# A decoder layer on one core: the value projection made wide, turned tiles sent through DRAM, weights loaded from GpSimd's queue, and another order of the value products

## The chip, the cores and the metric

The kernel runs on one core of a Trainium2 chip. The metric is the device time of one execution in microseconds, lower is better. The engines are named as the profile names them: PE is TensorE (PEld its weight loads), DVE is VectorE, ACT is ScalarE, POOL is GpSimd, and SP is SyncE, which here only issues DMAs.

## The reference, cut to what matters

The reference is one decoder layer over 2048 tokens of width 1024, in float32. The input is normalised and multiplied by one large matrix, whose columns give the inputs of two groups of heads. The first group has four HGRN2 heads: a recurrence whose state is a 128 x 128 matrix for each head. The second has eight attention heads of width 64 over two key and value heads, with a window of 128 tokens and a learned sink in the softmax. Both outputs are normalised or weighted, joined, multiplied by an output matrix and added to the input. Then follow a gated MLP with a causal convolution of three taps, a residual sum and a last normalisation.

```python
u = rmsnorm(h, norm_mix_w)
proj = u @ w_in                      # hq, hf, hi, hg and the attention's q, k, v
# an HGRN2 head, token by token, with k_t = 1 - f_t and v_t from hi:
#   S_t = diag(f_t) S_(t-1) + k_t v_t^T,   o_t = S_t^T q_t
# an attention head:
p = jnp.exp(scores - m)
denom = jnp.sum(p, axis=-1, keepdims=True) + jnp.exp(sink - m)
out = jnp.einsum('bnhgqk,bnkhd->bnqhgd', p / denom, vb)
```

The change concerns `hi`, the values of the HGRN2 heads (512 of the columns of `w_in`), and the way in which some tiles are turned from tokens on partitions to features on partitions or back.

## The kernel before, in words

The 2048 tokens are worked in two halves of 1024. In each half the mixing stage comes first (projections, HGRN2 heads, attention), then the output projection, the gate and up projections, and the down projection.

The normalised input lies in SBUF with the 1024 features on partitions, eight tiles of 128 x 1024 tokens. Each tile is kept as two parts, XH (rounded to the format of fast float32 products) and XL (what the rounding left). A weight is split in the same way: `prep` (L192) loads 128 x 1024 floats (512 KB) into `raw`, a ring of three buffers, by a DMA of SP (L198); ACT casts it to the high part (L199, whi), DVE subtracts (L200, wlo). The two parts have rings of two buffers each. A projection of 128 columns is a `unit` (L203): 48 products of 128 x 512 (L218), that is eight feature tiles, three combinations of high and low parts, and two blocks of 512 tokens, into two PSUM banks. The ring `mm` of PSUM banks has four.

The HGRN2 values are not a `unit`. `project_v` (L670) works on two heads at once: for each of eight tiles of 128 tokens it makes 24 products of 128 x 256 (L681 to L683), with the tokens' tile as the stationary operand and the weight as the moving one, so that the result `pvv` has tokens on partitions. ACT copies it out in 16 activations that scale each token by its `rs` (L685). There are 192 such products in a call, 768 in the program.

The order of the mixing stage is a list, `ORDER` (L40). Its entries are f, q, l, s, p for an HGRN2 head (forget gate, query, seven levels, state, product), qa, sc, pv, pw for a pair of attention heads (query projection, scores and softmax, value products of the first and of the second block of 512 tokens), v for a value projection, g for a gate and m for a split. The list is the order in which the code is written; a scheduler then settles the order on each engine, so that neighbouring stages mix. Within one engine, and on SP's and POOL's queues, the settled order is kept: an instruction that waits holds up those behind it.

A level of an HGRN2 head multiplies the tiles Q and K by gates on DVE (L564, L565), makes small products on PE (plev, L558 and L572), and copies part of them under a mask into ST (L584). ST is cleared first by a memset of POOL (L507). The levels' small products are float32 and stand between the wide products of whichever projection runs at the time.

The attention's softmax tile `sc` has queries on partitions; its value products need keys there. For pairs 0 to 2 `turned` (L335) turns it: DVE transposes blocks of 32 x 32 (L338), and SP issues 16 DMAs of 32 KB from SBUF to SBUF (L341) that put the blocks in their places in `pt`. Then DVE picks out the part of `pt` that belongs to a block's own tokens (po, L453), and PE makes the value products (poT, L471) from `pt` and `po`. The outputs of heads 0 to 2 (`on`) are turned by the same function into `hg`. Pair 3 and head 3 are turned by PE instead. So there are 12 tiles `pt` and 6 tiles `hg` in the program.

Of the kernel before, what the change touches and what calls it, by code (L numbers as in the profile page):

```python
# [17 lines left out]
P = 128  # L18
# [20 lines left out]
UP_AFTER = 'T2'  # L39
ORDER = ("f0 q0 l0 qa0 v0 sc0 s0 p0 f1 q1 pv0 pw0 l1 qa1 sc1 f2 s1 p1 q2 pv1 pw1 l2 qa2 v1 sc2 f3 s2 p2 q3 pv2 "  # L40
         "pw2 l3 qa3 sc3 s3 p3 pv3 pw3 g0 g1 m4 m5 m6 g2 m0 m1 g3 m7 m2 m3").split()
LEVELS = [1, 2, 4, 8, 16, 32, 64]
# [4 lines left out]
TURNED_PAIRS = 3  # L47
TURNED_HEADS = 3


@with_exitstack
def hymba_layer(ctx: ExitStack, tc: tile.TileContext, a: dict, out: bass.AP, rows_out: bass.AP):
# [139 lines left out]
    def prep(src, slots=False, parts=(slice(0, D),)):  # L192

        raw = raw4(None)
        hi, lo = [hp.tile([P, D], F32R, tag="m", name=f"w{t}", bufs=KT) if slots else
                  wp.tile([P, D], F32R, tag=t, name=f"w{t}", bufs=2) for t in ("hi", "lo")]
        for c in parts:
            nc.sync.dma_start(raw[:, c], src[:, c])  # L198
            nc.scalar.copy(hi[:, c], raw[:, c])  # L199
            nc.vector.tensor_tensor(lo[:, c], raw[:, c], hi[:, c].bitcast(F32), op=ALU.subtract)  # L200
        return hi, lo
# [132 lines left out]

    def turned(p, tag, bufs, src, dst):  # L335

        t = p.tile([P, 4, 8, 32], F32, tag=tag, name="turn", bufs=bufs)
        nc.vector.transpose(t, src.rearrange("p n (c j) -> p c n j", j=32))  # L338
        for a in range(4):
            for c in range(4):  # L340
                nc.sync.dma_start(dst[32 * c:32 * c + 32, a], t[32 * a:32 * a + 32, c])  # L341

    def rows(kv):
        return slice(kv * HD, (kv + 1) * HD)
# [38 lines left out]
    def attend(hf, j, X, invb, KS, V, VD, mix, p):  # L383
# [9 lines left out]
        for g in range(NB):  # L393
# [48 lines left out]
            if j < TURNED_PAIRS:  # L442
                pt = p.tile([P, 4, 8, 32], F32, tag="sc", name="pt", bufs=2)
                turned(p, "pp", 3, sc.rearrange("p a b c -> p (a b) c"), pt)
                sc = pt
# [39 lines left out]
    def hgrn(hf, h, X, invb, vs, WG, gates, mix, p, fu=None):  # L485
# [114 lines left out]
        kept = TT if hf + 1 < NH else TT - 1  # L600
        Kn = p.tile([P, TT, P], F32, tag="t4", name="Kn", bufs=2)
        for b in range(NB):
            pk = ps("hg", "pkn")
            n = min(4, kept - 4 * b)
            for i in range(n):
                c = slice((b * 4 + i) * P, (b * 4 + i + 1) * P)
                nc.tensor.transpose(pk[:, i * P:(i + 1) * P], K[:, c], ident)
            nc.scalar.copy(Kn[:, 4 * b:4 * b + n].rearrange("p a b -> p (a b)"), pk[:, 0:n * P])
        SS = p.tile([P, TT, P], F32, tag="SS", name="SS", bufs=1)
        for b in range(NB):  # L610
            pu = ps("hg", "pu")
            for c in range(4 * b, min(4 * b + 4, kept)):
                i = c % 4
                marks["pu"] = nc.tensor.matmul(pu[:, i * P:(i + 1) * P], Kn[:, c], v[:, c], start=True, stop=True)
            for c in range(4 * b, min(4 * b + 4, kept)):
# [13 lines left out]
        for b in range(NB):  # L629
            at = [po[b][:, i * P:(i + 1) * P] for i in range(4)]  # L630
            empty = hf == 0 and b == 0
            for i in range(4):
                for k in range(2):
                    marks["po"] = nc.tensor.matmul(at[i][rows(k)], ST[:, k, 4 * b + i], v[:, 4 * b + i],
                                                   start=i == 0, stop=empty and i == 0, skip_group_check=True)
# [15 lines left out]
        if h < TURNED_HEADS:  # L651
            turned(p, "t4", 2, on, q.rearrange("p (a c q) -> p a c q", a=4, c=TT))
        for b, bs in halves() if h >= TURNED_HEADS else ():
# [15 lines left out]

    def project_v(hf, pr, X, rs, p):  # L670

        v = [p.tile([P, TT, P], F32, tag="v", name="v", bufs=VB) for _ in range(2)]
        parts = [prep(a["w_v"][pr, s]) for s in range(2)]
        for tt in range(TT):
            o = ps("mm", "pvv")
            t = slice(tt * P, (tt + 1) * P)
            for kt in range(KT):
                hi, lo = parts[kt // 4]
                xh, xl = X[kt]
                c = slice((kt % 4) * 256, (kt % 4 + 1) * 256)  # L680
                nc.tensor.matmul(o[:, 0:256], xh[:, t], hi[:, c], start=kt == 0, stop=False)  # L681
                nc.tensor.matmul(o[:, 0:256], xl[:, t], hi[:, c], start=False, stop=False)  # L682
                nc.tensor.matmul(o[:, 0:256], xh[:, t], lo[:, c], start=False, stop=kt == KT - 1)  # L683
            for i in range(2):
                nc.scalar.activation(v[i][:, tt], o[:, i * P:(i + 1) * P], AF.Identity, scale=rs[:, tt:tt + 1])  # L685
        return v
# [467 lines left out]
    for hf in range(NH):  # L1154
        X, kv, invb, rs, f0 = nxt
        with ExitStack() as st:
# [7 lines left out]
            for name in ORDER:  # L1164
# [9 lines left out]
                elif stage == "v":  # L1174
                    vs += project_v(hf, n, X, rs, p)
                else:
# [10 lines left out]
def _layout(i):  # L1187
# [3 lines left out]
    def cols(w, idx):  # L1191
# [12 lines left out]
    w_out = i["w_out"][0][np.concatenate(rows)]  # L1204
    w_v = np.stack([cols(w_in, 1024 + pr * 256 + ar(256)).reshape(P, 2, D).transpose(1, 0, 2) for pr in range(2)])
    conv = np.concatenate([i["conv_w"][0], i["conv_b"]], 0)
# [5 lines left out]
        "w_f": np.stack([cols(w_in, 512 + h * P + ar(P)) for h in range(4)]),  # L1212
        "w_v": w_v,
        "w_g": np.stack([cols(w_in, 1536 + h * P + ar(P)) for h in range(4)]),
# [39 lines left out]
```

## Time and profile before

| | |
|---|---|
| time, median of 3 runs | 2129.19 us (2128.93 to 2129.2) |
| time of the profiled execution | 2129.44 us |
| span of its trace | 2127.7 us |
| TensorE clock granted in the profiled execution | 0.999 of full speed |
| TensorE busy | 99% of the span |
| VectorE, ScalarE, GpSimd busy | 77%, 49%, 1% |

The span runs from the first instruction of the trace to the last, 1.7 us less than the execution's own time. In a row of the timeline the first number is the start in us from the span's start, the second how long the row lasts, then engine, line, operation, the tiles written and read, the shape, and after x the number of instructions that the row joins; brackets hold the idle time of the engine just before it and what ended that. Durations of products on TensorE overlap: the next starts before the last has drained. SPq is SP's queue, where a row lasts as long as the issue takes; the DMA itself lands later, and the list of DMA issues gives the count, the KB of each and the median us from issue to landing.

### The profile page before, as it was taken

What the parts mean: (1) busy time and instruction counts of PE and PEld (TensorE: products, weight loads), DVE (VectorE), ACT (ScalarE), POOL (GpSimd) and SP (SyncE); (2) the same over time, 40 slices, a digit from 0 to 9 for tenths busy, and PEclk for the clock granted to TensorE, in tenths of its full rate; (3) what the DMA queues carried; (4) which work ended last, traced back from release to release, by engine and by line L of the source; (5) the groups of instructions that cost most, each with busy time, mean ns of one, the idle gap of its engine ahead of it and who ended that gap; (6) DMA issues with size and microseconds to landing.
All of it is one profiled execution on the core that took longest, in us unless ns stands there. A gap on an engine that the chain in (4) does not pass through costs nothing.

```text
span 2127.7 us, 30275 instructions
## 1 busy us (share of the span) xinstructions
PE 2113.7 (99%) x11575; PEld 1763.0 (83%) x11575; DVE 1632.4 (77%) x2427; ACT 1050.0 (49%) x1855; POOL 16.9 (1%) x43
## 2 busy tenths in 40 slices
PE   8999999999999999999999999999999999999998
PEld 6988888888888888888889898888888888888887
DVE  6587786798887878785865776867988788887765
ACT  5455645564444445335635456555544444453353
POOL 2000000000000000000000000000000000000000
PEclk9999999999999999999999999999999999999999
DMA  4121213413232335964641212242223323259644
GB/s 162 42 59 45 68 52 102 136 59 121 91 124 92 98 116 168 379 235 150 216 143 40 61 38 64 60 146 97 80 99 103 110 90 124 94 194 403 228 149 134
DMA packets 105810, 264.34 MB, mean 124 GB/s; under 512 B 15808, under 2 KB 28608, under 8 KB 105664
## 3 DMA queue, kind: packets, MB, share of 16 engines
q1 hardware_dynamic: 105232, 262.14, 36.6%
q8 instruction: 91, 1.49, 0.3%
q14 instruction: 55, 0.45, 0.1%
q10 hardware_dynamic: 432, 0.27, 0.0%
HBM read 195.56 MB, written 57.34 MB: 119 GB/s over the span
## 4 chain that ended last, share of the span: by engine, by line
PE 97%; DVE 2%; DMA 1%; ACT 0%; issue 0%; SPq 0%; ACTq 0%; DVEq 0%
PE X L818 7%; PE X L816 7%; PE X L817 7%; PE pop L218 7%; PE hq L218 4%; PE q L218 4%; PE g L218 4%; PE f L218 4%; PE Y L817 4%; PE Y L818 4%; PE Y L816 4%; PE pdx L1004 3%; PE pdx L1003 3%; PE pdx L1005 3%; PE pdy L1004 3%; PE pdy L1003 3%
## 5 line engine op out<-in xcount | busy, mean ns | idle before, releaser
L689 ACT CAST whi<-raw 128x1024 fp32r<-128x1024 f32 x88 | 92.7, 1053 | 115.1 <-PE X L817 73.1
L816 PE MATMUL X<-T,whi 128*128 128x512 f32 x352 | 136.9, 389 | 0.0
L817 PE MATMUL X<-T,whi 128*128 128x512 f32 x352 | 136.9, 389 | 0.0
L818 PE MATMUL X<-T,wlo 128*128 128x512 f32 x352 | 136.9, 389 | 0.0
L887 DVE SCALAR_TENSOR_TENSOR y<-ga,cw,y 128x1024 f32<-128x1024 f32 x88 | 112.5, 1279 | 25.9 <-ACT y L885 25.9
L822 ACT COPY u<-X 128x512 f32<-128x512 f32 x88 | 51.5, 585 | 122.8 <-PE X L818 122.6
L690 DVE TENSOR_TENSOR wlo<-raw,whi 128x1024 fp32r<-128x1024 f32 x88 | 107.2, 1218 | 4.4 <-ACT whi L689 4.4
L199 ACT CAST whi<-raw 128x1024 fp32r<-128x1024 f32 x58 | 60.6, 1050 | 89.9 <-PE pop L218 36.7
L690 DVE TENSOR_TENSOR xld<-raw,xhd 128x1024 fp32r<-128x1024 f32 x72 | 80.9, 1131 | 18.3 <-ACT xhd L689 18.2
L689 ACT CAST xhd<-raw 128x1024 fp32r<-128x1024 f32 x72 | 70.0, 978 | 37.6 <-DMA raw<-act0T 12.0
L218 PE MATMUL pop<-XL,whi 128*128 128x512 f32 x256 | 82.8, 390 | 0.0
L218 PE MATMUL pop<-XH,wlo 128*128 128x512 f32 x256 | 82.6, 390 | 0.0
L218 PE MATMUL pop<-XH,whi 128*128 128x512 f32 x256 | 82.5, 391 | 0.0
L200 DVE TENSOR_TENSOR wlo<-raw,whi 128x1024 fp32r<-128x1024 f32 x58 | 70.5, 1217 | 10.4 <-ACT whi L199 10.1
L818 PEld LDWEIGHTS X<-T,wlo 128*128 128x128 f32 x352 | 66.1, 188 | 13.8
L817 PEld LDWEIGHTS X<-T,whi 128*128 128x128 f32 x352 | 66.1, 188 | 13.7
L816 PEld LDWEIGHTS X<-T,whi 128*128 128x128 f32 x352 | 66.0, 188 | 13.7
L682 PE MATMUL pvv<-whi,XL 128*128 128x256 f32 x256 | 72.7, 285 | 0.0
L681 PE MATMUL pvv<-whi,XH 128*128 128x256 f32 x256 | 72.6, 285 | 0.0
L683 PE MATMUL pvv<-wlo,XH 128*128 128x256 f32 x256 | 72.4, 287 | 0.0
L818 PE MATMUL X<-B,wlo 128*128 128x512 f32 x176 | 68.7, 390 | 0.8 <-DVE wlo L690 0.8
L817 PE MATMUL X<-T,Sh 128*128 128x512 f32 x176 | 68.6, 390 | 0.5 <-DVE T L690 0.5
(388 smaller groups left out, 6287.9 us busy)
## 6 DMA issues: line engine op xcount, KB each, us to landing
wr<-in_w_down SPq DMA_DIRECT2D x90, 512.0 KB, 5.6
raw<-in_w_gate SPq DMA_DIRECT2D x44, 512.0 KB, 3.6
raw<-in_w_up SPq DMA_DIRECT2D x44, 512.0 KB, 3.6
raw<-act0T SPq DMA_DIRECT2D x20, 512.0 KB, 5.6
raw<-act1T SPq DMA_DIRECT2D x20, 512.0 KB, 5.9
act0B<-y SPq DMA_DIRECT2D x33, 256.0 KB, 2.4
act1B<-y SPq DMA_DIRECT2D x33, 256.0 KB, 2.4
raw<-in_w_out SPq DMA_DIRECT2D x16, 512.0 KB, 3.7
```

The lines of the kernel that those rows point to most:

```text
L218: nc.tensor.matmul(o[b], w, x[:, bs], start=f, stop=l)
L681: nc.tensor.matmul(o[:, 0:256], xh[:, t], hi[:, c], start=kt == 0, stop=False)
L682: nc.tensor.matmul(o[:, 0:256], xl[:, t], hi[:, c], start=False, stop=False)
L683: nc.tensor.matmul(o[:, 0:256], xh[:, t], lo[:, c], start=False, stop=kt == KT - 1)
L689: nc.scalar.copy(h, src)
L690: return (eng or nc.vector).tensor_tensor(l, src, h.bitcast(F32), op=ALU.subtract)
L816: nc.tensor.matmul(o, wh[:, ws], xh, start=i == 0 and not more, stop=False, skip_group_check=more)
L817: nc.tensor.matmul(o, wh[:, ws], xl, start=False, stop=False, skip_group_check=more)
L818: nc.tensor.matmul(o, wl[:, ws], xh, start=False, stop=i == 3, skip_group_check=more)
L887: nc.vector.scalar_tensor_tensor(y, g[:, w:w + HALF], C.cw[:, ft, w:w + 1], y, op0=ALU.mult, op1=ALU.add)
L1003: nc.tensor.matmul(o, wh[:, i, c], ah[:, i, cols], start=f, stop=False, skip_group_check=more)
L1004: nc.tensor.matmul(o, wh[:, i, c], al[:, i, cols], start=False, stop=False, skip_group_check=more)
```

## The change

The value projection is now a `unit` for one head: 48 products of 128 x 512 with the weight as the stationary operand, 384 in the program. Its result `vT` has the head's 128 features on partitions and lies in two PSUM banks. DVE transposes both banks in blocks of 32 x 32, the tile goes through `turned` into `v`, and eight activations of ACT scale it in place. `v` is laid out as 4 groups of 32 features with the token tiles between them, and the products that read it (pu and po of the HGRN2 heads) take it in four pieces of 32 elements.

`turned` makes one DMA of 512 KB from SBUF into a DRAM tile (`turned`, four buffers) and four DMAs of 128 KB back, each for 32 partitions. It serves 26 tiles: the 12 `pt`, the 6 `hg` and 8 `v`. SP's 288 transfers of turned tiles become 130: 26 writes, 48 reads of `pt`, 24 of `hg`, 32 of `v`.

`prep` issues its DMA from POOL's queue where it was SP's. That concerns 58 loads; the weights of gate, up and down are loaded elsewhere and stay with SP.

`ORDER` has four v entries where it had two, in other places, and for pairs 0 to 2 the value products stand behind the levels of the next head; for pairs 0 and 1 they stand behind the next pair's query projection too. A branch for turned keys is added and is not taken (`TURNED_KEYS` is 0). In the changed kernel the lines behind `turned` are numbered some ten higher (L453 is L463, L471 is L481, L584 is L594), those of `prep` one higher.

```diff
-ORDER = ("f0 q0 l0 qa0 v0 sc0 s0 p0 f1 q1 pv0 pw0 l1 qa1 sc1 f2 s1 p1 q2 pv1 pw1 l2 qa2 v1 sc2 f3 s2 p2 q3 pv2 "
-         "pw2 l3 qa3 sc3 s3 p3 pv3 pw3 g0 g1 m4 m5 m6 g2 m0 m1 g3 m7 m2 m3").split()
+ORDER = ("f0 q0 l0 qa0 v0 v1 sc0 s0 p0 f1 q1 l1 qa1 pv0 pw0 sc1 f2 s1 p1 q2 l2 qa2 v2 pv1 pw1 v3 sc2 f3 s2 p2 q3 l3 pv2 pw2 qa3 sc3 s3 p3 pv3 pw3 g0 g1 m4 m5 m6 g2 m0 m1 g3 m7 m2 m3").split()
...
+DB = 4
...
-            nc.sync.dma_start(raw[:, c], src[:, c])
+            nc.gpsimd.dma_start(raw[:, c], src[:, c])
...
-    def turned(p, tag, bufs, src, dst):
+    def turned(p, tag, bufs, src, dst, strided=False):
 
         t = p.tile([P, 4, 8, 32], F32, tag=tag, name="turn", bufs=bufs)
-        nc.vector.transpose(t, src.rearrange("p n (c j) -> p c n j", j=32))
-        for a in range(4):
-            for c in range(4):
-                nc.sync.dma_start(dst[32 * c:32 * c + 32, a], t[32 * a:32 * a + 32, c])
+        tv = t.rearrange("p c n i -> p c (n i)").rearrange("p c (i n) -> p c n i", n=8) if strided else t
+        for i, s in enumerate(src):
+            n = 8 // len(src)
+            nc.vector.transpose(tv[:, :, i * n:(i + 1) * n], s.rearrange("p (n c j) -> p c n j", n=n, j=32))
+        d = dp.tile([P, 4, 256], F32, tag="turned", name="turned", bufs=DB)
+        nc.sync.dma_start(d.rearrange("p c x -> p (c x)"), flat(t))
+        for c in range(4):
+            nc.sync.dma_start(dst[32 * c:32 * c + 32].rearrange("p a b c -> p a (b c)"),
+                              d[:, c].rearrange("(a j) x -> j a x", a=4))
...
-                marks["pu"] = nc.tensor.matmul(pu[:, i * P:(i + 1) * P], Kn[:, c], v[:, c], start=True, stop=True)
+                marks["pu"] = nc.tensor.matmul(pu[:, i * P:(i + 1) * P], Kn[:, c], v[:, :, c], start=True, stop=True)
...
-    def project_v(hf, pr, X, rs, p):
-
-        v = [p.tile([P, TT, P], F32, tag="v", name="v", bufs=VB) for _ in range(2)]
-        parts = [prep(a["w_v"][pr, s]) for s in range(2)]
-        for tt in range(TT):
-            o = ps("mm", "pvv")
-            t = slice(tt * P, (tt + 1) * P)
-            for kt in range(KT):
-                hi, lo = parts[kt // 4]
-                xh, xl = X[kt]
-                c = slice((kt % 4) * 256, (kt % 4 + 1) * 256)
-                nc.tensor.matmul(o[:, 0:256], xh[:, t], hi[:, c], start=kt == 0, stop=False)
-                nc.tensor.matmul(o[:, 0:256], xl[:, t], hi[:, c], start=False, stop=False)
-                nc.tensor.matmul(o[:, 0:256], xh[:, t], lo[:, c], start=False, stop=kt == KT - 1)
-            for i in range(2):
-                nc.scalar.activation(v[i][:, tt], o[:, i * P:(i + 1) * P], AF.Identity, scale=rs[:, tt:tt + 1])
+    def project_v(h, X, rs, p):
+
+        o = unit(a["w_v"][h], X, "vT")
+        v = p.tile([P, 4, TT, 32], F32, tag="v", name="v", bufs=VB)
+        turned(p, "pp", 3, o, v)
+        for c in range(TT):
+            nc.scalar.activation(v[:, :, c], v[:, :, c], AF.Identity, scale=rs[:, c:c + 1])
         return v
```

The scheduler's order moves in the whole mixing stage. Three places show what the prediction speaks of.

The first is VectorE in the first half, from the softmax of pair 0's second block on. Before, the names are: `sc` the softmax tile, `turn` its blocks transposed, `po` the first and then the second block's own part, K, Q, ST and F the levels of the next head.

```order
L441 TENSOR_TENSOR sc<-sc,den 128x1024
L338 STREAM_TRANSPOSE turn<-sc 128x1024
L453 TENSOR_TENSOR po<-pt,ownT 128x1024
L565 TENSOR_TENSOR Q<-Q,F_1455 128x2x64x4
L584 COPY_PREDICATED ST<-lmask_297,plev 64x2x32x4 x2
L564 TENSOR_TENSOR K<-K,F_1489 128x2x16x16
L490 TENSOR_TENSOR f<-f_1771,invb 128x512
L490 TENSOR_TENSOR f<-f_1772,invb 128x512
L200 TENSOR_TENSOR wlo<-raw,whi 128x1024
L419 MEMSET sc 128x128 x2
L565 TENSOR_TENSOR Q<-Q,F_1472 128x2x32x8
L584 COPY_PREDICATED ST<-lmask_303,plev 64x2x16x8 x2
```

The po of the second block stands four rows behind the last of these, after three small products of F. In the changed kernel, from the same multiplication on:

```order
L451 TENSOR_TENSOR sc<-sc,den 128x1024
L575 TENSOR_TENSOR Q<-Q,F_1305 128x2x64x4
L594 COPY_PREDICATED ST<-lmask_297,plev 64x2x32x4 x2
L346 STREAM_TRANSPOSE turn<-sc 128x1024
L463 TENSOR_TENSOR po<-pt,ownT 128x1024
L574 TENSOR_TENSOR K<-K,F_1339 128x2x16x16
L575 TENSOR_TENSOR Q<-Q,F_1322 128x2x32x8
L594 COPY_PREDICATED ST<-lmask_303,plev 64x2x16x8 x2
L429 MEMSET sc 128x128 x2
L463 TENSOR_TENSOR po<-pt,ownT 128x1024
L500 TENSOR_TENSOR f<-f_1639,invb 128x512
L500 TENSOR_TENSOR f<-f_1640,invb 128x512
```

The transpose now has the level's Q and masked copies ahead of it instead of behind it, and the second block's po (the second L463) stands five rows behind the first where it stood thirteen behind.

The second is TensorE at the same pair: `poT` are the value products, hq and f are projections of the next heads, plev a level's small products. Before, at the start of the second block:

```order
L218 MATMUL hq_1938<-XL,whi 128x512
L218 MATMUL hq_1937<-XH,wlo 128x512
L558 MATMUL plev<-Q,G 64x2x32 x8
L218 MATMUL hq_1938<-XH,wlo 128x512
L471 MATMUL poT<-pt,V 64x128 x2
L218 MATMUL hq_1937<-XH,whi 128x512
L218 MATMUL hq_1938<-XH,whi 128x512
L414 MATMUL psc<-KS,qx 128x128
L218 MATMUL hq_1937<-XL,whi 128x512
L471 MATMUL poT<-po,VD 64x128 x2
L471 MATMUL poT<-pt,V 64x128 x2
```

In the changed kernel, from the end of the first block's products on:

```order
L219 MATMUL f_1639<-XL,whi 128x512
L219 MATMUL f_1640<-XL,whi 128x512
L219 MATMUL f_1639<-XH,wlo 128x512
L219 MATMUL f_1640<-XH,wlo 128x512
L219 MATMUL hq_1795<-XH,whi 128x512
L568 MATMUL plev<-Q,G 64x2x32 x8
L219 MATMUL hq_1796<-XH,whi 128x512
L219 MATMUL hq_1795<-XL,whi 128x512
L219 MATMUL hq_1796<-XL,whi 128x512
L481 MATMUL poT<-pt,V 64x128 x2
L219 MATMUL hq_1795<-XH,wlo 128x512
L219 MATMUL hq_1796<-XH,wlo 128x512
```

The second block begins (poT<-pt) after nine rows of other work behind the first block, where it stood 25 rows behind before; the wide products around it are the same kind.

The third is SP's queue in the first half, where weights, turned tiles of pairs 0 and 1 (`pt`) and of head 0 (`hg`) follow each other. Before:

```order
L373 DMA kcarry<-KS 256x1x128
L374 DMA vcarry<-V 128x128
L198 DMA raw<-in_w_q 128x1024
L198 DMA raw<-in_w_att 128x1024
L198 DMA raw<-in_w_f 128x1024
L198 DMA raw<-in_w_q 128x1024
L198 DMA raw<-in_w_att 128x1024
L341 DMA pt<-turn 32x256 x16
L341 DMA hg_537<-turn 32x256 x16
L198 DMA raw<-in_w_v 128x1024 x2
L341 DMA pt<-turn 32x256 x16
L198 DMA raw<-in_w_f 128x1024
```

In the changed kernel, from the same two rows on:

```order
L383 DMA kcarry<-KS 256x1x128
L384 DMA vcarry<-V 128x128
L348 DMA turned<-turn 128x1024
L350 DMA v<-turned 32x4x256 x4
L348 DMA turned<-turn 128x1024
L350 DMA v<-turned 32x4x256 x4
L348 DMA turned<-turn 128x1024
L350 DMA pt<-turned 32x4x256 x4
L348 DMA turned<-turn 128x1024 x2
L350 DMA pt<-turned 32x4x256 x4
L350 DMA hg_537<-turned 32x4x256 x4
```

The weights are gone from SP, the tiles `v` are new, and a write of one tile can stand ahead of the reads of another. The weights' loads are now on POOL, here from its masks (`lmask`) at the start of the program on:

```order
L117 AFFINE_SELECT lmask_297<-lmask_297 128x64 x2
L117 AFFINE_SELECT lmask_303<-lmask_303 128x64 x2
L199 DMA raw<-in_w_f 128x1024
L117 AFFINE_SELECT lmask_309<-lmask_309 128x64 x2
L119 AFFINE_SELECT lmask_285<-lmask_285 128x64 x2
L119 AFFINE_SELECT lmask_291<-lmask_291 128x64 x2
L119 AFFINE_SELECT lmask_297<-lmask_297 128x64 x2
L119 AFFINE_SELECT lmask_303<-lmask_303 128x64 x2
L119 AFFINE_SELECT lmask_309<-lmask_309 128x64 x2
L199 DMA raw<-in_w_q 128x1024
L199 DMA raw<-in_w_att 128x1024
L199 DMA raw<-in_w_v 128x1024 x2
```

Before, POOL had no load; here the first f weight stands between the selects, the others behind them, and the memset of the first ST behind the second f weight.

More of the change, by code (lines that the diff above doesn't have):

```diff
@@ L48 @@
 TURNED_HEADS = 3
+TURNED_KEYS = 0
+DB = 4
 @with_exitstack
@@ L333, in across, with flat @@
         return bass.AP(v.tensor, v.offset + base, [list(v.ap[0])] + dims)
-    def turned(p, tag, bufs, src, dst):
+    def flat(t):
+        return t.rearrange("p a b c -> p (a b c)")
+    def turned(p, tag, bufs, src, dst, strided=False):
         t = p.tile([P, 4, 8, 32], F32, tag=tag, name="turn", bufs=bufs)
-        nc.vector.transpose(t, src.rearrange("p n (c j) -> p c n j", j=32))
-        for a in range(4):
-            for c in range(4):
-                nc.sync.dma_start(dst[32 * c:32 * c + 32, a], t[32 * a:32 * a + 32, c])
+        tv = t.rearrange("p c n i -> p c (n i)").rearrange("p c (i n) -> p c n i", n=8) if strided else t
[7 more added lines that the diff above has]
+                              d[:, c].rearrange("(a j) x -> j a x", a=4))
     def rows(kv):
@@ L443, in attend @@
                 pt = p.tile([P, 4, 8, 32], F32, tag="sc", name="pt", bufs=2)
-                turned(p, "pp", 3, sc.rearrange("p a b c -> p (a b) c"), pt)
+                turned(p, "pp", 3, [sc.rearrange("p a b c -> p (a b c)")], pt)
                 sc = pt
@@ L600, in hgrn @@
         kept = TT if hf + 1 < NH else TT - 1
-        Kn = p.tile([P, TT, P], F32, tag="t4", name="Kn", bufs=2)
-        for b in range(NB):
+        if h < TURNED_KEYS:
+            Kt = p.tile([P, 4, 32, TT], F32, tag="t4", name="Kt", bufs=2)
+            turned(p, "t4", 2, [K], Kt, True)
+            Kn = Kt.rearrange("p a i n -> p n (a i)")
+        else:
+            Kn = p.tile([P, TT, P], F32, tag="t4", name="Kn", bufs=2)
+        for b in range(NB) if h >= TURNED_KEYS else ():
             pk = ps("hg", "pkn")
@@ L633, in hgrn @@
                 for k in range(2):
-                    marks["po"] = nc.tensor.matmul(at[i][rows(k)], ST[:, k, 4 * b + i], v[:, 4 * b + i],
+                    marks["po"] = nc.tensor.matmul(at[i][rows(k)], ST[:, k, 4 * b + i], v[:, :, 4 * b + i],
                                                    start=i == 0, stop=empty and i == 0, skip_group_check=True)
@@ L651, in hgrn @@
         if h < TURNED_HEADS:
-            turned(p, "t4", 2, on, q.rearrange("p (a c q) -> p a c q", a=4, c=TT))
+            turned(p, "t4", 2, [on.rearrange("p c t -> p (c t)")], q.rearrange("p (a c q) -> p a c q", a=4, c=TT))
         for b, bs in halves() if h >= TURNED_HEADS else ():
@@ L1174, in hymba_layer @@
                 elif stage == "v":
-                    vs += project_v(hf, n, X, rs, p)
+                    vs.append(project_v(n, X, rs, p))
                 else:
@@ L1204, in _layout @@
     w_out = i["w_out"][0][np.concatenate(rows)]
-    w_v = np.stack([cols(w_in, 1024 + pr * 256 + ar(256)).reshape(P, 2, D).transpose(1, 0, 2) for pr in range(2)])
     conv = np.concatenate([i["conv_w"][0], i["conv_b"]], 0)
@@ L1212, in _layout @@
         "w_f": np.stack([cols(w_in, 512 + h * P + ar(P)) for h in range(4)]),
-        "w_v": w_v,
+        "w_v": np.stack([cols(w_in, 1024 + h * P + ar(P)) for h in range(4)]),
         "w_g": np.stack([cols(w_in, 1536 + h * P + ar(P)) for h in range(4)]),
```

## The prediction

> **What bounds the kernel now.** I read the page's engine line first, then its chain of waits, then the waits of TensorE, then the timeline at the places that the change touches.
>
> ```profile
> PE 2113.7 (99%) x11575; PEld 1763.0 (83%) x11575; DVE 1632.4 (77%) x2427; ACT 1050.0 (49%) x1855; POOL 16.9 (1%) x43
> PE 97%; DVE 2%; DMA 1%; ACT 0%; issue 0%; SPq 0%; ACTq 0%; DVEq 0%
> PE kv L218 <- ACT XH L232: 5.5, 1, 5.5
> PE X L818 <- DVE wlo L690: 0.8, 2, 0.4
> PE X L817 <- DVE T L690: 0.5, 1, 0.5
> PE kv L218 <- DVE XL L233: 0.3, 1, 0.3
> PE poT L471 <- DVE po L463: 0.2, 1, 0.2
> ```
>
> TensorE is busy for 99% of the span, the chain runs through it for 97%, and its own waits come to 7.3 us in 2127.7. So nothing can be gained here but TensorE work, and nothing lost but new TensorE work or a new wait of TensorE. SP's queue, VectorE and ScalarE matter only where they make TensorE wait. Of its five waits one belongs to the value products (poT), and it is 0.2 us long: those products come just in time.
>
> **The value projection.** It gives up 768 products of 128x256 (pvv) for 384 of 128x512 (vT), the form that f has today. The durations in the rows overlap, so I take the distance of starts, from the timeline of TensorE inside an f unit and a pvv unit:
>
> ```profile
> 35.41 0.62 PE L218 MATMUL f<-XH,whi 128*128 128x512 f32 x2
> ...
> 42.20 0.61 PE L218 MATMUL f<-XH,whi 128*128 128x512 f32 x2
> 188.31 0.28 PE L681 MATMUL pvv<-whi,XH 128*128 128x256 f32 x1
> ...
> 190.10 0.28 PE L681 MATMUL pvv<-whi,XH 128*128 128x256 f32 x1
> ```
>
> The f rows hold two products each, so the two shown are 30 apart: 6.79 / 30 = 226.3 ns. The pvv rows are 15 apart: 1.79 / 15 = 119.3 ns. So 768 x 119.3 = 91.6 us go and 384 x 226.3 = 86.9 us come: **-4.7 us**, all of it TensorE time. The Trainium skill, "TensorE: Matmul & The Clock Gate", section "Back-to-back issue gap", gives N / 2.4 + 2.5 ns for isolated products; by that I estimate 109.2 and 215.8 ns, and the exchange would save only 1.0 us and the total would come out 3.7 us higher. The trace disagrees by some 10 ns at both widths, and it shows exactly the two forms exchanged, so it decides.
>
> The evacuation moves: ScalarE keeps 64 small activations, VectorE gets 16 transposes of half the size of today's 1.24 us (row below), about 10 us in two halves, while it is idle for 23% of the span. Their cover is the bank ring: four banks, so a unit of 48 products (10.9 us) runs before a vT bank is wanted again. Without that cover each late transpose would cost TensorE up to 0.6 us.
>
> **Small products between wide ones.** The scheduler's order differs all over the mixing stage, and each visit to the small float32 products (levels, value products) costs something at entry and exit:
>
> ```profile
> 154.76 0.39 PE L218 MATMUL hq<-XH,whi 128*128 128x512 f32 x1
> 155.08 0.44 PE L471 MATMUL poT<-po,VD 128*64 128x128 f32 x4
> 155.35 0.39 PE L471 MATMUL poT<-pt,V 128*64 128x128 f32 x4
> 155.56 0.39 PE L471 MATMUL poT<-po,VD 128*64 128x128 f32 x4
> 157.22 0.50 PE L218 MATMUL hq<-XH,whi 128*128 128x512 f32 x1
> 157.56 0.62 PE L218 MATMUL hq<-XL,whi 128*128 128x512 f32 x2
> ```
>
> Entry takes 0.32 us where 0.226 is the rule, the first four 0.27 against 0.21, the exit 0.34 against 0.226: 0.26 us for a visit. I count 82 visits in the order of before and 85 after, with value products in 33 pieces where there were 27. Three visits are +0.8 us; where a piece lies against other small products it costs nothing, and a few merge, down to -0.2. I take **+0.5 us**.
>
> **The turned tiles.** Today a transpose is followed by 16 transfers. VectorE, then SP, then TensorE, for pair 0 of the first half:
>
> ```profile
> 148.61 1.25 DVE L338 STREAM_TRANSPOSE turn<-sc 128x1024 f32<-128x1024 f32 x1
> ...
> 150.88 0.68 DVE L565 TENSOR_TENSOR Q<-Q,F 128x512 f32<-128x512 f32 x1
> 151.59 0.90 DVE L584 COPY_PREDICATED ST<-lmask,plev 64x256 f32<-64x256 uint32 x2
> 162.07 1.22 DVE L453 TENSOR_TENSOR po<-pt,ownT 128x1024 f32<-128x1024 f32 x1 [1.72 <-DMA pt<-turn]
> 149.88 10.63 SPq L341 DMA_DIRECT2D pt<-turn  x16
> 132.16 1.11 PE L414 MATMUL psc<-KS,qx 128*128 128x256 f32 x8
> 163.48 0.44 PE L471 MATMUL poT<-pt,V 128*64 128x128 f32 x4
> L338 DVE STREAM_TRANSPOSE turn<-on x6: 1187/1235/1246, 127.4 to 1334.6; 128x1024 f32<-128x1024 f32 x6
> ```
>
> The transpose ended at 149.86; SP needed 10.6 us for the issues, and VectorE's next op on the tile began at 162.07: a trip of 12.2 us. TensorE's product on it came at 163.48, 1.4 us after the landing. The new trip is one write of 512 KB and four reads of 128 KB. Its rows:
>
> ```profile
> keep<-h SPq DMA_DIRECT2D x32, 256.0 KB, 2.1
> raw<-in_w_gate SPq DMA_DIRECT2D x44, 512.0 KB, 3.6
> pt<-turn SPq DMA_DIRECT2D x192, 32.0 KB, 1.8
> KS<-kcarry SPq DMA_DIRECT2D x1, 128.0 KB, 3.6
> ```
>
> A write of 512 KB to DRAM is not in the trace; it lies between 2.1 (half the size, the same way) and 3.6 (the same size, the other way). A read of 128 KB lies between 1.8 and 3.6. An issue is 0.66 us (10.63 / 16) for 32 partitions, 0.33 in the rows of weights below. So the trip is 2.1 + 3 x 0.33 + 1.8 = 4.9 us at best and 0.7 + 3.6 + 4 x 0.66 + 3.6 = 10.5 at worst; I take 2.8 + 3 x 0.5 + 2.7 = **7.0 us**, nearer to the rows of the same kind.
>
> That is 5 us less than now, but the new order has spent it. For pair 0 of the first half I count, from the last score product to the first second-block value product, 87 wide products where 104 stood: 17 x 226.3 = 3.8 us less cover. VectorE has 4.4 us more to do between the same scores and their transpose: head 0's output tile (a multiply of some 1.2 us and its transpose, 1.24), one Q (0.68), two masked copies (0.90), small ones (0.4); 0.9 us of idle time there can take some. So the trip may last 12.2 + 1.4 - 3.8 - 4.4 + 0.9 = 6.3 us before TensorE waits. By the same count pair 0 of the second half leaves 6.2 us, the other four places 8.7 to 11. With 7.0 us that is 0.7 + 0.8, **+1.5 us** of waits, where before had 0.2. With 4.9 it is none; with 10.5 it is 4.2 + 4.3 and some 3.8 at the others, 12.3.
>
> VectorE will wait longer than its 1.72 us in front of the second po, since only 3.7 us of work is left between transpose and po (12.2 us before, the wait among it). Queued behind po are f's scaling, qx and Q, 3.9 us with po, and the next small level product needs that Q; TensorE has 4.0 us between the landing and that product, so this adds no second wait. The first-block tiles and the v tiles have some 30 us or more and cost nothing. The 288 small issues that leave SP, and the 130 that come, cost nothing by themselves: no row of TensorE's waits names SP.
>
> **Weights by GpSimd's queue.** 58 loads of 512 KB leave SP. No GpSimd load is in the trace, so I bound it by what each load has in hand. The tightest two, from SP's and ScalarE's timelines (first f weight, then the second half's first attention weight):
>
> ```profile
> 19.39 0.33 SPq L198 DMA_DIRECT2D raw<-in_w_f  x1
> 30.63 2.00 ACT L199 CAST whi<-raw 128x1024 fp32r<-128x1024 f32 x2 [3.69 <-PE kv L218]
> 1045.36 0.33 SPq L198 DMA_DIRECT2D raw<-in_w_att  x1
> 1055.41 1.03 ACT L199 CAST whi<-raw 128x1024 fp32r<-128x1024 f32 x1
> raw<-in_w_f SPq DMA_DIRECT2D x8, 512.0 KB, 3.6
> 10.00:15.00 5.00, 4.84 (x17) 2.82 (x16) 3.73 (x5) 4.59 (x6) 3.31 (x7) 1.00 1.03 418
> 2.78 4.99 POOL L116 TENSOR_SCALAR_AFFINE_SELECT lmask<-lmask 128x64 f32<-128x64 f32 x10
> ```
>
> From issue to cast are 11.2 and 10.0 us, of which 3.6 is the transfer: 7.6 and 6.4 in hand. The first cast waited for TensorE, not for its load. On GpSimd the first f weight stands after eight of the first ten selects, at about 6.8 us, while x is still loading and the transfer engines are full (share 1.03): it may hold up x, and so the first 5.5 us wait. I take **+0.3 us**, between 0 and 1.3. The memsets of ST are now queued among these loads; each stands behind loads whose buffers come free, in VectorE's order, well ahead of that ST's first use, so none shows.
>
> **The sum.** 2129.44 (profiled execution, span 2127.7 and 1.7 around it) - 4.7 + 0.5 + 1.5 + 0.3 = 2127.0; the median of the runs lies 0.25 lower, so **2126.8 us**. That is 0.11% faster. I call 0.2% (4.3 us, from 2124.9 to 2133.4) about what a measurement of this kernel can tell from no change.
>
> **The rivals.**
>
> A, the gain arrives whole. The trip is 6 us or less, the visits merge, x is not disturbed: 2129.2 - 4.7 - 0.2 + 0.1 = 2124.4. For it: the low end of the trip, and the orders priced by the distances of starts leave visits near nothing. Against it: the two places with 6.2 and 6.3 us.
>
> B, slower: the DRAM trip is late at the second-block value products. One mechanism, six places. At 10.5 us the waits are 12.3, and the time 2129.2 - 4.7 + 0.5 + 0.3 + 12.3 = 2137.6. It decides from a trip of about 9.6 us, where the waits reach 8 us. For it: the write must land before the reads start, so two transfers add up where 16 overlapped, and weights may be moving at the same time. Against it: a wait at one place gives VectorE time to catch up.
>
> C, slower too: GpSimd's loads are late. If they needed 10 us more than SP's, the two starts would lose 2.4 + 3.6 us, and x 1.3 more: with my waits about 2133.8. The Trainium skill, "SBUF — State Buffer", section "Who interferes with whom", says that a load issued from GpSimd can be held while VectorE runs a copy or tensor_scalar in a two-port mode. No run here shows it yet. VectorE's rows above are tensor_tensor and masked copies, so I see little that would hold a load for 6 us.
>
> **Chances.** My forecast 0.45, its own range 2124.9 to 2131; A 0.33; B 0.17; C 0.05. So faster 0.33, within 0.2% 0.45, slower 0.22. The range from 2123.5 to 2135.0 takes in A and the lower part of B, and leaves out most of B above it and a little below A.
>
> **What would show it.** Starts of vT 226 ns apart, 384 of them. From the end of a score transpose to the next po of its tile 7 us, with VectorE waiting about 3 us there. In TensorE's waits a poT row that names the DMA pt<-turned, 1 to 2 us in sum, most of it at pair 0 of either half; 8 us or more would be B, none A. No wait of TensorE that ends on a weight's cast; the first wait for XH still near 5.5 us. I am wrong if the vT starts are further apart, if a wait turns up at vT's banks or at pu behind the v tiles, or if GpSimd's loads take much longer than 3.6 us.

## The result, and the profile after

The changed kernel takes 2141.53 us (median of 4 runs, 2139.08 to 2145.48) where the kernel before takes 2129.19: ratio 1.006, 95% interval 1.0042 to 1.0077. That is 12.3 us slower, and outside the range given. The profiled execution, 2139.08 us, is the lowest of the four. Its page's engine line and chain of waits:

```profile
PE 2116.0 (99%) x11191; PEld 1740.7 (81%) x11191; DVE 1640.5 (77%) x2443; ACT 1050.2 (49%) x1855; POOL 46.6 (2%) x101
PE 89%; DVE 5%; DMA 3%; ACT 2%; issue 1%; SPq 1%; DVEq 0%; ACTq 0%
```

TensorE's waits (line, what it waited for, us in total, times, longest):

```profile
PE kv L219 <- ACT XH L233: 5.7, 2, 5.5
PE psc L424 <- ACT qx L414: 3.0, 2, 2.3
PE poT L481 <- DMA pt<-turned: 1.7, 2, 1.4
PE X L823 <- DVE T L696: 1.1, 1, 1.1
PE X L824 <- DVE wlo L696: 0.8, 2, 0.4
PE psc L424 <- ACT att L485: 0.8, 1, 0.8
PE pkn L622 <- ACT ST L601: 0.6, 1, 0.6
PE psc L424 <- DVE sc L433: 0.5, 1, 0.5
PE kv L219 <- DVE XL L234: 0.4, 2, 0.3
```

TensorE still looks 99% busy, but its share of the chain fell from 97% to 89%. The largest new waits name ScalarE: scores (psc) wait for qx and att. The wait that my second rival was built on (poT for the DMA) is there too, with 1.7 us.

What ScalarE was doing then, from its timeline (in brackets its idle time and what ended it):

```profile
94.42 2.45 ACT L691 ACTIVATE v<-v,y 128x128 f32<-128x128 f32 x8 [12.24 <-DMA v<-turned]
...
227.23 0.62 ACT L412 CAST qx<-att 64x512 fp32r<-64x512 f32 x1
236.02 2.44 ACT L691 ACTIVATE v<-v,y 128x128 f32<-128x128 f32 x8 [8.17 <-DMA v<-turned]
238.49 0.62 ACT L414 CAST qx<-qx 64x512 fp32r<-64x512 f32 x1
```

SP's queue ahead of the second of these waits:

```profile
220.06 1.66 SPq L348 DMA_DIRECT2D turned<-turn  x3
222.77 2.48 SPq L350 DMA_DIRECT2D pt<-turned  x4
225.76 2.06 SPq L350 DMA_DIRECT2D hg<-turned  x4
227.86 2.68 SPq L350 DMA_DIRECT2D v<-turned  x4
```

The scaling of v stands in ScalarE's queue ahead of the cast of qx, and waits 8.17 us for its tile. SP had issued that tile's write as the last of three from 220.06 on, but its reads stand behind those of pt and hg, and go out from 227.86 on. The whole program has 37.9 us of such waits:

```profile
ACT v L691 <- DMA v<-turned: 37.9, 6, 12.2
```

What TensorE felt of it, from its timeline:

```profile
236.22 0.69 PE L582 MATMUL plev<-Q,K 128*64 128x64 f32 x16
239.16 1.00 PE L424 MATMUL psc<-KS,qx 128*128 128x128 f32 x3 [2.25 <-ACT qx L414]
239.96 1.05 PE L219 MATMUL f<-XL,whi 128*128 128x512 f32 x2
241.81 1.22 PE L424 MATMUL psc<-KS,qx 128*128 128x256 f32 x4 [0.79 <-ACT att L485]
```

The windows of the wait and of what followed (the window, its length, busy time and count of PE, PEld, DVE, ACT and POOL, then the granted clock, the DMA share and GB/s):

```profile
237.00:239.20 2.20, 0.04 (x1) 0.04 (x1) 0.00 (x0) 2.15 (x8) 0.00 (x0) 0.97 0.38 111
239.20:246.00 6.80, 6.01 (x17) 4.61 (x18) 2.16 (x4) 6.64 (x18) 0.00 (x0) 0.51 0.18 45
```

A wait of 2.25 us and a second of 0.79, and between and behind them TensorE ran at half its clock (0.51) for nearly 7 us: the pair of f products at 239.96 lasts 1.05 us where such pairs last 0.62. Together this one place costs some 5.6 us: 3.0 of waits, 10 wide products at 0.2 us more each and 7 scores at some 0.1 us more each.

To see where all the time is, I add up the distances between the starts of successive products of TensorE: between wide (or narrow) products, at the edges between these and the small ones or scores, and among the small ones (a few transposes by TensorE, `rows` and `pv`, are counted with the wide ones). A distance over 0.45 us counts as a wait, less 0.23 for the product itself. In us:

| | wide and narrow | edges | among small | waits |
|---|---|---|---|---|
| before | 1905.9 | 48.0 | 157.7 | 3.8 |
| wide alone (e5) | 1899.8 | 50.5 | 157.9 | 7.2 |
| DRAM trip alone (e6) | 1906.7 | 48.4 | 157.0 | 7.2 |
| order alone (e7) | 1905.9 | 50.4 | 157.5 | 4.7 |
| changed | 1901.6 | 50.4 | 160.9 | 12.1 |

The first two columns belong together: a distance holds the time of the product that it starts from, and edges that started from a narrow product now start from a wide one. Together they fall by 1.9 us with the half-clock products in them, so most of the projection's gain is there. Against it stand 8.3 us of waits and 3.2 us among small products. That is the 9.6 us between the two profiled executions; for the other 2.7 us of the 12.3 there is no trace.

### The profile page after: what moved, and what is told of

Same layout as the page of the kernel before. It is cut to its first block, busy times and chain, and to the rows that moved or that the text cites. A ratio compares the mean times of both kernels' runs of the same rounds, so it can differ in the third digit from the quotient of the medians.

```text
span 2137.4 us, 29405 instructions
## 1 busy us (share of the span) xinstructions
PE 2116.0 (99%) x11191; PEld 1740.7 (81%) x11191; DVE 1640.5 (77%) x2443; ACT 1050.2 (49%) x1855; POOL 46.6 (2%) x101
## 4 chain that ended last, share of the span: by engine, by line
PE 89%; DVE 5%; DMA 3%; ACT 2%; issue 1%; SPq 1%; DVEq 0%; ACTq 0%
PE X L824 7%; PE X L822 7%; PE X L823 7%; PE pop L219 7%; PE Y L823 4%; PE Y L824 4%; PE Y L822 4%; PE hq L219 4%; PE q L219 3%; PE g L219 3%; PE pdx L1010 3%; PE pdx L1009 3%; PE pdx L1011 3%; PE vT L219 3%; PE pdy L1009 3%; PE pdy L1010 3%
## 5 line engine op out<-in xcount | busy, mean ns | idle before, releaser
L823 PE MATMUL X<-T,Sh 128*128 128x512 f32 x176 | 68.7, 390 | 1.1 <-DVE T L696 1.1
L822 PE MATMUL X<-T,Sh 128*128 128x512 f32 x176 | 68.7, 390 | 0.0
L822 PE MATMUL Z<-B,whi 128*128 128x512 f32 x176 | 68.7, 390 | 0.0
L822 PE MATMUL X<-B,whi 128*128 128x512 f32 x176 | 68.7, 390 | 0.0
```

What stands on the lines that cost most here:

```text
L822: nc.tensor.matmul(o, wh[:, ws], xh, start=i == 0 and not more, stop=False, skip_group_check=more)
L823: nc.tensor.matmul(o, wh[:, ws], xl, start=False, stop=False, skip_group_check=more)
```

## The experiments

Theory Q is the one read above: ScalarE's queue is held by scalings whose v tile has not landed. Its rivals: T, the trip of the second-block tiles; G, late loads from GpSimd; O, the new order. Each run has a median of 5 to 11 executions, with the kernel before beside it (2129.26 to 2129.73 us).

| run | us | ratio to before, 95% interval |
|---|---|---|
| e1 scaling on VectorE | 2146.43 | 1.0083 (1.0069 to 1.0097) |
| e2 weights on SP | 2141.76 | 1.0058 (1.0045 to 1.0070) |
| e3 small transfers for scores and outputs | 2138.37 | 1.0042 (1.0030 to 1.0055) |
| e4 old order | 2142.32 | 1.0058 (1.0045 to 1.0071) |
| e5 wide alone | 2128.36 | 0.9997 (0.9988 to 1.0005) |
| e6 DRAM trip alone | 2132.44 | 1.0016 (1.0007 to 1.0025) |
| e7 order alone | 2132.78 | 1.0017 (1.0008 to 1.0026) |
| e8 GpSimd alone | 2129.59 | 1.0001 (0.9992 to 1.0010) |
| e9 v not turned | 2134.84 | 1.0026 (1.0017 to 1.0036) |
| e10 as e2, v scaled on GpSimd | 2133.21 | 1.0021 (1.0012 to 1.0030) |
| e11 as e5, scores earlier | 2128.41 | 0.9996 (0.9987 to 1.0005) |
| e12 v's whole path on GpSimd | 2140.96 | 1.0056 (1.0043 to 1.0068) |
| e13 v scaled on GpSimd, nothing else | 2136.97 | 1.0042 (1.0028 to 1.0055) |
| e14 as e10, old order | 2136.36 | 1.0033 (1.0021 to 1.0044) |
| e15 as e14, small transfers | 2140.39 | 1.0053 (1.0040 to 1.0065) |

**e1**, on the changed kernel:

```diff
+        for b, bs in halves():
+            nc.vector.tensor_tensor(o[b], o[b], rs[:, bs], op=ALU.mult)
         turned(p, "pp", 3, o, v)
-        for c in range(TT):
-            nc.scalar.activation(v[:, :, c], v[:, :, c], AF.Identity, scale=rs[:, c:c + 1])
...
-                    vs.append(project_v(n, X, rs, p))
+                    vs.append(project_v(n, X, invb, p))
```

> The changed kernel, but the scaling of v is taken off ScalarE: VectorE multiplies each vT bank by the inverse norm (invb) in place in PSUM before the transpose, two more VectorE operations of 128x512 for each head; everything else as changed. Theory Q (ScalarE's queue: the eight in-place scalings stand in it before their tile has landed, 37.9 us of waiting, and hold up qx and the casts behind them): the excess of TensorE between 85 and 110 us, between 229 and 250 us and near 1314 us goes, some 8 us with the half-clock stretch, so about 2133 us; the waits psc<-qx vanish. Theory T (the trip of the second-block tiles through DRAM): those waits stay and so does the time, 2140 us or a little more for the added VectorE work. Theory G (late loads from GpSimd's queue): no change either.

2146.43 us: slower still, by 5 us. The waits for qx shrank to 0.7 us, but others came. TensorE's timeline in the same stretch:

```profile
220.82 0.69 PE L568 MATMUL plev<-Q,G 128*64 128x64 f32 x16 [1.23 <-DVE Q L575]
225.64 1.12 PE L568 MATMUL plev<-Q,G 128*64 128x64 f32 x16 [4.13 <-DVE Q L575]
228.21 1.07 PE L582 MATMUL plev<-Q,K 128*32 128x32 f32 x32 [1.45 <-DVE Q L575]
231.15 0.80 PE L219 MATMUL f<-XH,whi 128*128 128x512 f32 x1 [1.88 <-DVE turn L346]
```

The levels now wait for VectorE's Q, and f for a bank that VectorE has yet to transpose. So this run removes one queue's wait and fills another queue. It does not speak against Q; it shows that VectorE had no room here. Call that theory V.

**e2**: `nc.gpsimd.dma_start` in `prep` is `nc.sync.dma_start` again.

> The changed kernel, with the 58 loads of prep back on SP's queue. Theory G: most of the 12 us loss goes, about 2130 us. Theory Q: the loads wait for nothing new, the time stays within 2 us of the changed kernel (2139 to 2145 us), or rises, since the turned tiles' reads on SP then stand behind loads that wait for a free buffer. Theory T: the same as Q.

2141.76 us, no change: theory G falls.

**e3**: the function of the kernel before turns the softmax tiles and head outputs, the new one only v.

```diff
-                turned(p, "pp", 3, [sc.rearrange("p a b c -> p (a b c)")], pt)
+                turned16(p, "pp", 3, sc.rearrange("p a b c -> p (a b) c"), pt)
...
```

> The changed kernel, with the softmax tiles and the head outputs turned by 16 small transfers from SBUF to SBUF as before; only the v tiles go through DRAM. Theory T: the second-block waits (poT and the loss near 159 and 1218 us, 2 to 3 us together in the profile) go, or more if the trip is the main cause: 2131 us or less. Theory Q: ScalarE still waits for the v tiles, and on SP their reads now stand behind 16 issues of 0.6 us for each other tile, so the time stays near 2141 us or rises to 2150 us.

2138.37 us: 3 us of the 12, between what T and Q expected. ScalarE still waits 31.4 us for v; in this order TensorE loses nothing near 236 us, but some 5 us near 1410 us, where the fourth pair's products wait for VectorE and ScalarE.

**e4**: in `ORDER` the value products are back ahead of the next head's levels, and v3 stands beside v2.

> The changed kernel, with the value products back in their old places (pv and pw ahead of the next head's levels; v0 v1 ahead of the first scores and v2 v3 ahead of the third, as the two-head calls stood). A theory O, that the new places of the value products cost the time: about 2131 us. Theory Q: the scalings still wait on ScalarE, the sum of those waits stays 25 us or more, and the time stays within 4 us of the changed kernel's 2141 us; how much of each wait TensorE feels depends on what stands behind it. Theory T: the trips get less cover or more, with 1 to 3 us of difference.

2142.32 us: theory O falls as the sole cause. The poT waits for the DMA rise to 5.8 us, in four places.

**e5** to **e8** make one part each on the kernel before. e5 makes a `unit` per head with ScalarE's evacuation straight from the banks, e6 has the new body of `turned`, e7 moves only the pv and pw entries, e8 issues `prep`'s loads from GpSimd.

```diff
+            o = unit(a["w_v"][2 * pr + i], X, "vT")
...
+                nc.scalar.activation(t[:, c], o[c // 4][:, (c % 4) * P:(c % 4 + 1) * P], AF.Identity, scale=rs[:, c:c + 1])
```

> The kernel before with the value projection alone made wide: 48 products of 128x512 for each head at the old places in the order, ScalarE's 16 evacuations of 128x128 for a pair of heads as before, SP's weights and small transfers as before. Left out is the turning: v stays with features on partitions. This is the first term of the sum by itself. By my sum 2129.2 - 4.7, or some 2 us more where the order's visits merge: 2122.5 to 2124.5 us. By theory W (the wide projection itself costs, because the narrow one spread work so that VectorE could catch up): 2128 us or more, with waits of TensorE for VectorE in the levels.

> The kernel before with only the turned tiles changed: one write to DRAM and four reads for the 12 softmax tiles and 6 head outputs. By my sum for a trip of 7 us against 12.2 and an order that spends the difference: 2129 to 2131 us. Theory T (the trip is the main cause): 2134 us or more, with poT waiting for DMA at several places. Theory Q: near 2129 us, since no instruction of ScalarE waits for such a tile.

> The kernel before with only the value products of pairs 0 to 2 moved behind the next head's levels (and behind the next query projection for pairs 0 and 1). The products priced by the distances of starts cost 0.4 us more. My sum gives this move nothing but the visits: 2129 to 2130 us. Theory O: 2135 us or more.

> The kernel before with only the 58 loads of prep on GpSimd's queue. By my sum +0.3 us, 2129 to 2130.5 us. Theory G: 2132 us or more, with a load's landing well above 4.2 us or a cast waiting for it.

e5 came to -1.0 us, within the noise, e6 to +3.1, e7 to +3.4, e8 to +0.3: together +5.8 us. e6 and e7 lie between the sum and the theory that their expectations set against it. In e5's profile (2130.0 us, the highest of its runs), 3.7 us of TensorE's waits are at the end of the first half's mixing stage or for softmax there:

```profile
PE poT L471 <- ACT pw L462: 1.9, 1, 1.9
PE po L634 <- DVE m L432: 1.4, 1, 1.4
PE poT L471 <- DVE po L463: 0.4, 1, 0.4
```

So e5 has the time that its expectation gave to theory W, but not W's waits, which were to be in the levels.

e6 shows theory T by itself, from TensorE's waits:

```profile
PE poT L473 <- DMA pt<-turned: 3.1, 3, 1.2
```

For e7 the table of distances says where: 2.4 us more at edges and 0.9 of waits.

**e9**, on the changed kernel, leaves out the turning of v:

```diff
-        turned(p, "pp", 3, o, v)
-            nc.scalar.activation(v[:, :, c], v[:, :, c], AF.Identity, scale=rs[:, c:c + 1])
+            nc.scalar.activation(v[:, :, c], o[c // 4][:, (c % 4) * P:(c % 4 + 1) * P].rearrange("p (a j) -> p a j", a=4), AF.Identity, scale=rs[:, c:c + 1])
```

> The changed kernel without the turning of v: ScalarE scales the vT banks straight into v (64 activations of the same size), with no transpose on VectorE and no DMA for v. Left out is the turning, so v keeps features on partitions. The parts by themselves came to -1.0 (wide), +3.1 (DRAM), +3.4 (order), +0.3 us (GpSimd), +5.8 together where the change cost 12.3. If the turning of v is the missing 6.5 us (its wait on ScalarE, its transposes on VectorE, its reads on SP), about 2135 us here, and the stretch from 229 to 250 us keeps its full clock. If the parts disturb each other in some other way, 2139 to 2142 us as changed.

2134.84 us, 5.6 above before: the medians of the four parts do add up, and the turning of v is the other 6.7 us. TensorE loses nothing near 236 us in its trace, and the clock is full there.

**e10**, on e2:

```diff
-        for c in range(TT):
-            nc.scalar.activation(v[:, :, c], v[:, :, c], AF.Identity, scale=rs[:, c:c + 1])
+        nc.gpsimd.tensor_tensor(v, v, rs.unsqueeze(1).unsqueeze(3).to_broadcast([P, 4, TT, 32]), op=ALU.mult)
```

> As e2 (the changed kernel with the weights back on SP), but v is scaled in place by one multiplication on GpSimd for each head, so that nothing in ScalarE's or VectorE's queue waits for a v tile; VectorE keeps its 16 transposes and no more. Theory Q (ScalarE's queue): psc<-qx and the half-clock stretch near 236 us go, 4 to 6 us less than e2: 2136 to 2138 us. Theory V (VectorE's 16 added transposes in a stretch where it is already full): the waits move to VectorE as in e1, and the time stays at 2141 us or more.

2133.21 us, 8.5 below e2 with intervals that don't touch. GpSimd now does the waiting, with nothing behind it that TensorE needs. Its timeline:

```profile
92.91 1.91 POOL L690 TENSOR_TENSOR v<-v,y 128x1024 f32<-128x1024 f32 x1 [77.92 <-DMA v<-turned]
105.55 1.92 POOL L690 TENSOR_TENSOR v<-v,y 128x1024 f32<-128x1024 f32 x1 [10.72 <-DMA v<-turned]
233.29 1.92 POOL L690 TENSOR_TENSOR v<-v,y 128x1024 f32<-128x1024 f32 x1 [124.77 <-DMA v<-turned]
```

The v tile still lands late (233.29 here, 236.02 as changed), VectorE still makes its transposes, and TensorE's waits for qx, 2.7 us in e2, are gone. That speaks for theory Q. But the loss near 236 us is not gone. TensorE's wait there, what ScalarE had waited for, and the window behind it (columns as above):

```profile
237.52 1.38 PE L424 MATMUL psc<-KS,qx 128*128 128x256 f32 x8 [1.97 <-ACT att L485]
235.60 0.61 ACT L411 CAST qx<-att 64x512 fp32r<-64x512 f32 x1 [3.23 <-DMA turned<-turn]
238.90:242.30 3.40, 3.40 (x10) 2.65 (x9) 1.09 (x3) 0.46 (x2) 1.91 (x1) 0.50 0.04 8
```

qx and the transposed tile `turn` take their buffers from one ring of three (`pp`). The next qx waited until the write of the next v tile to DRAM, issued at 230.17, had landed at 235.53, and the copy to att stood behind it in ScalarE's queue. So the turning of v holds ScalarE in a second way, by its buffer: call that theory R. ScalarE waits for such a write for 3.7 us in e10, 6.3 in e13 and 7.7 in e1; in the changed kernel the scalings hide it. No run tests R by itself. Nor is all of e10's gain located: by the table's rule its profile has 5.9 us less of waits than e2's, and poT's waits for the DMA, which fall from 3.9 to 1.5 us, are part of that.

**e11**, on e5: `qa3 pv2 pw2 sc3 q3 l3` where `q3 pv2 pw2 l3 qa3 sc3` stood.

> As e5 (the kernel before with the wide projection alone, v not turned), with the fourth pair's query projection and scores moved ahead in the list (qa3 pv2 pw2 sc3 q3 l3 s3 p3 where q3 pv2 pw2 l3 qa3 sc3 s3 p3 stood). Theory E (the end of the mixing stage: in e5's first half the scheduler put the fourth pair's last scores 10 us of TensorE work ahead of its last transposes, where before had 23 us, and softmax on VectorE and ScalarE isn't ready): here 27 us lie between them, the waits poT<-pw and po<-m near 347 to 357 us go, and the time is 2124 to 2126 us. If the loss in e5's first half has another cause, 2128 us or more.

2128.41 us. The waits of e5's profile for pw and m are gone and TensorE's waits are 4.5 us by the table's rule, but the time is e5's. The edges rose to 52.0 us, which gives 1.5 of the 2.7 us back. Theory E explains one profile, not the medians.

**e12** to **e15** look for a version to use. e12 has the wide projection, v's write, reads and scaling on GpSimd, all else as before. e13 is the changed kernel with e10's edit alone, e14 is e10 with the old order, e15 is e14 with the small transfers too.

> A version to use: wide projection, v turned through DRAM with its write, its reads and its scaling all on GpSimd's queue, weights and all other turned tiles as before (SP, 16 small transfers), value products at their old places. The products priced by the distances of starts cost 6.4 us less than before; v waits hold up nobody's queue but GpSimd's. If the v path was the cost through the queues that it shared: 2124 to 2128 us. If VectorE's 16 transposes cost by themselves (theory V): 2131 us or more, with TensorE waiting for VectorE in the levels.

> The changed kernel with one edit: v is scaled in place by one GpSimd multiplication for each head (1.9 us in e10) and not by ScalarE. The weights stay on GpSimd's queue, so the loads behind a multiplication wait for the v tile too. Theory Q (ScalarE's queue held by the v tiles is the 6.7 us that the parts don't add up to): 2133 to 2136 us, no psc<-qx wait and full clock near 240 us. If e10's gain came from the weights' queue together with it: 2139 us or more.

> As e10 (v scaled on GpSimd, weights on SP), with the value products back at their old places. The order alone cost 3.4 us on the kernel before. If that adds up: 2129 to 2131 us. If the old places are worse beside the DRAM trip, as e4 against the changed kernel suggests (2142.3 against 2141.5): 2133 us or more.

> As e14, and the softmax tiles and head outputs turned by 16 small transfers as before, so that only the wide projection and the turning of v through DRAM are left of the change. The DRAM trip of those tiles alone cost 3.1 us. If it adds up: 2126 to 2129 us. If VectorE, which has 10 us more to do, is late in the levels as in e12 (which differs in having the v transfers on GpSimd's queue): 2136 us or more, with plev waiting for VectorE's Q.

e13: 2136.97 us, 4.6 below the changed kernel by one edit; its interval and the changed kernel's overlap, 0.6 us of waits for qx and 1.7 for att remain near 236 us, and 2.1 us of its waits are for pw at the end of the second half's stage. Why it gains less than e10, from which only the weights' queue differs, is not shown. e14: 2136.36, not the 2129 to 2131 that adding would give. e12 and e15 are at 2141 and 2140 us, for another reason, which TensorE's waits in e15 show:

```profile
PE plev L576 <- DVE Q L583: 8.2, 4, 3.2
```

The window of 200 to 220 us in the kernel before, columns as above:

```profile
200.00:220.00 20.00, 20.00 (x234) 19.07 (x233) 19.03 (x42) 11.18 (x43) 0.00 (x0) 1.00 0.19 52
```

VectorE was busy for 19.03 of these 20 us before anything was added. In these two orders its Q comes late for the levels. So theory V is what the traces of e1, e12 and e15 name. For the changed kernel the runs show that the turning of v costs 6.7 us, and that taking its scaling off ScalarE (Q) wins 4.6 to 8.5 us; R is seen and not separated. No version beat the kernel before clearly; e5 and e11 are level with it and leave out the turning.

## Why the prediction was wrong

**The wide products** were priced rightly and paid less. In the changed kernel's timeline the vT pairs start as the f pairs did:

```profile
203.98 0.62 PE L219 MATMUL vT<-XH,wlo 128*128 128x512 f32 x2
...
208.06 0.61 PE L219 MATMUL vT<-XH,wlo 128*128 128x512 f32 x2
```

18 products in 4.08 us, 226.7 ns. The visits, which I took at +0.5 us, are not where the gain went. The edges rise by 2.4 us in the changed kernel and 2.5 in e5, but 30 of the 269 edges before start from a narrow product (0.189 us on average, where those from a wide one take 0.274), and that product's own time is in the exchange already. The edges even fall in number, to 259 and 261, where I had counted three more visits. In the two traces TensorE's work in e5 falls by 3.6 us with the edges in it, with 3.4 us at half clock near 356 us, where I had 4.2; but 3.4 us of new waits take it back there. My sum had no such waits; in e5's median the -4.7 became -1.0.

**The step that failed** is one sentence on the v tiles: that they "have some 30 us or more and cost nothing". I counted from the transpose to pu, the first product that reads v. The first reader is ScalarE's scaling. I did note that ScalarE "keeps 64 small activations", and took the same number for the same cost; but before they read a bank that was full, and now a tile that comes by DMA. The change had added a wait, and I did not ask what stands behind it in ScalarE's queue: qx, and so the scores. e9 puts the turning of v at 6.7 us, and e10 and e13 take 8.5 and 4.6 us off with the scaling alone. My count also left out that the transposed v tile keeps a buffer, in the ring that qx uses, until its write has landed (R); what that costs alone stays open.

**The DRAM trip** was right in kind and low in length. The second-block trips, from transpose to VectorE's po, took 7.2 to 9.6 us (7.0 taken), with the write at 2.7 and the reads at 3.0:

```profile
turned<-turn SPq DMA_DIRECT2D x26, 512.0 KB, 2.7
pt<-turned SPq DMA_DIRECT2D x48, 128.0 KB, 3.0
v<-turned SPq DMA_DIRECT2D x32, 128.0 KB, 4.2
```

The waits that name it are 1.7 us where I had 1.5, at pair 0 of either half as foretold. VectorE waited 10.5 us in front of po in six places, where I had named about 3 us for one. Alone, in e6, the trip costs 3.1 us. My rival B had the right sign by the wrong mechanism: it needed 8 us at these places.

**The order** I gave nothing but visits; alone it costs 3.4 us (e7), and in the other direction, beside the DRAM trip (e4, e14), it gives nothing back. Why these don't add up stays open: each edit makes the scheduler place everything anew.

**VectorE's 10 us** I hid behind its 23% of idle time, a mean over the whole span. Around 200 to 220 us it had 5%. In the changed kernel the transposes found room, in e1, e12 and e15 more work or another order did not.

**GpSimd's queue** was right: +0.3 us taken, +0.25 measured (e8), which is within the noise, with loads landing in 4.0 to 4.5 us in the median where SP's took 3.6 to 3.9. Rival C did not happen: no wait of TensorE names a load. Whether VectorE held any of them is not shown.

## What to carry to other kernels

When an evacuation becomes a round trip, find the first instruction that reads the landed tile and list what is queued behind it on that engine: that queue, not the last reader's due time, is what the trip has to beat. List also who needs the buffer that the tile leaves from, since it is held until the write has landed. Give such a wait to an engine whose queue holds nothing urgent. And judge added work by the engine's idle time in the stretch where it lands, not by its share of the span.

## What the runs showed of the hardware

A gap of 2.25 us in TensorE's work was followed by nearly 7 us at half its granted clock (0.51), while the gap of 1.36 us at 1219 us left it at 1.00; here 3.0 us of waits cost some 5.6. The Trainium skill, "TensorE: Matmul & The Clock Gate", section "HAM oscillation — how this bites in real kernels", warns of idle gaps over some 3.4 us; here a shorter one did it, with small products ahead of it.

The length of a gap alone does not decide. In e14 a gap of 1.25 us at 1503.6 us was followed by 3.4 us at half clock (0.50), in e3 one of 1.94 us at 1417.2 us by none (1.00). In every trace of this case the clock changes only at whole steps of 3.41 us: the half-clock stretches inside the program last 3.4, 6.8 or 10.2 us. I cut each trace into these steps and took those at full clock, without the first and last 15 us. All 13 steps in which TensorE was busy for less than 0.43 of the time were followed by half clock; of the 8 between 0.43 and 0.58, one (e14's); of the more than 10,000 above that, none. So it counts how much of one step a gap fills.

A GpSimd multiplication of 128x1024 takes 1.92 us.
